# Normalising forgetting-attention heads on the output instead of on the probabilities, for six heads of eight

## The chip, the core and the metric

The kernel runs on one core of a Trainium2 chip. A core has a matrix engine (TensorE, PE in the profile, with its weight loads shown apart as PEld), a vector engine (VectorE, DVE), a scalar engine (ScalarE, ACT), GpSimd (POOL) and SyncE (SP), which here only starts DMAs. The metric is the device time of one execution, in microseconds (us). Lower is better.

## The reference

Two layers, each a feed-forward block, a mixer and a second feed-forward block on 512 tokens of width 1024, in float32. Half of the mixer's heads are forgetting-attention heads (FoX, eight of width 64), the other half differential-attention heads (Diff, four with two score maps each). Only the FoX heads are touched here:

```
s_f = einsum('bhqd,bhkd->bhqk', qf, k_f) * scale_f
s_f = s_f + cf[..., :, None] - cum_f[..., None, :]      # cumulative log forget gates
p_f = softmax(where(causal, s_f, -inf), axis=-1)
o_f = einsum('bhqk,bhkd->bhqd', p_f, v_f)
```

The outputs of all heads are concatenated, multiplied by `w_out` and added to the residual stream. A softmax is an exponential divided by its row sum; since the division is by one number per query, it can be done on the probabilities or on the output of the second product.

## The kernel before, in words

Every large product is made of three matmuls: each factor is split into a rounded high half and a remainder, and high x high, high x low and low x high are added in PSUM (`mm3`, L401 to L403 in the feed-forward and output products, L679 to L681 for the values). The halves come from one copy on ACT (L83) and one subtraction on DVE (L84). Weights stream from DRAM through a ring of tiles, loaded by SP and split as they come.

The mixer (called once per layer) puts its attention work in steps, one head after another: `units` is four Diff heads and then eight FoX heads, and each has four steps, one per block of 128 queries (`qb`) or keys (`kb`). The loop over `s` at the end of `mixer` does in step `s`:

- `trans_step`, for the head that is one unit and a step behind: PE transposes the probabilities of key block `kb` (L888) into a PSUM tile of tag "b", of which there are five; ACT copies the rounded half (L897) and DVE subtracts it (L898).
- `softmax_step`: two matmuls per score tile and one that adds the mask (L838, L839, L841), again into a "b" tile; DVE adds the cumulative gates and finds the row extreme (L874); ACT takes the exponential and, with `accum_out`, its row sum (L876); DVE takes the reciprocal of the sum (L877); ACT multiplies the block by it in place (L878).
- `pv_step`, one step behind `trans_step`: two matmuls against the value halves (L927, L928). After `kb` = 3 the two halves of a head's output sit on different partitions: ACT copies one (L957), DVE adds the other (L958) into `fo["u"]`, a [128, 512] tile that holds two heads, the even one on partitions 0 to 63. After the odd head `split_o` makes the two halves for the output product (L909 on ACT, L910 on DVE).

Between these, `fill_to` lets a generator of other PE work advance to a count written out by hand in `TARGET`: the remaining projections, the values, the gates, and at last the output product of finished heads (`out_early`). The probabilities of two units lie in two tiles `pg` of 2048 columns: columns 0 to 1279 for the four blocks of a unit, 1280 to 1791 for a second map or `fo["u"]`, and 1792 to 2047 unused. Small working tiles come from `t_tile`, a rotation of six.

The order in which an engine runs its instructions is not the order of the program text: the framework builds it ahead of time from the dependencies. On each engine it is then fixed, and an instruction that waits holds up what stands behind it.

The Diff heads already use a way by DRAM for their own norm (`diff_norm`): SP writes a row of numbers to DRAM (L976) and reads it back onto all partitions (L980), and DVE multiplies by it (L982). POOL's DMA queue (L134) carries loads that add onto a tile, for the feed-forward blocks only.

Of the kernel before, what the change touches and what calls it, by code (L numbers as in the profile page):

```python
# [8 lines left out]
F32 = mybir.dt.float32  # L9
F32R = mybir.dt.float32r  # L10
BF16 = mybir.dt.bfloat16
AF = mybir.ActivationFunctionType
ALU = mybir.AluOpType
AX = mybir.AxisListType

P = 128
S = 512
# [5 lines left out]
FOX_H = 8  # L23
DIFF_H = 4
NB = S // P
# [22 lines left out]
def rf(t):  # L48
    return t.bitcast(F32)
# [3 lines left out]
def trunk(ctx, tc, xT, x, gains, gain_row, w_gu, w_dn, w_in, w_ff, w_out, fbias, lams, subln, consts, rope, out):  # L53
    nc = tc.nc
    act, dve, pool, pe, sp = nc.scalar, nc.vector, nc.gpsimd, nc.tensor, nc.sync
# [3 lines left out]
    sm = ctx.enter_context(tc.tile_pool(name="sm", bufs=4))  # L59
    ps = ctx.enter_context(tc.tile_pool(name="ps", bufs=1, space=bass.MemoryType.PSUM))  # L60
    dram = ctx.enter_context(tc.tile_pool(name="dram", bufs=2, space=bass.MemoryType.DRAM))
    turn = {}

    def nxt(key, n):
        i = turn.get(key, 0)
        turn[key] = i + 1
        return i % n
# [4 lines left out]
    def home(tag, shape, dt, name):  # L72
        return sb.tile(shape, dt, tag=tag, name=name, bufs=1)

    def t_tile(shape, dt, name, i=None):
        return home(f"t{nxt('t', 6) if i is None else i}", shape, dt, name)
# [139 lines left out]
    for n in range(2 * DEPTH):  # L216
        l = n // 2
        if n % 2 == 1:
            for i in range(24 + len(OUT_K)):
                k = OUT_K[i - 24] if i >= 24 else None  # L220
                tag = MIX[i % 3] if i < 24 else None if k >= 4 else MIX[(i - 28) % 3]
# [44 lines left out]
    ident = const.tile([P, P], F32, name="ident")  # L266
# [328 lines left out]
    def mixer(l, n_next, mid):  # L595
# [11 lines left out]
        pg = [home(f"G{3 + i}", [P, 2048], F32, f"pg{i}") for i in range(2)]  # L607
        PR = {3: 0, 2: 512, 1: 896, 0: 1152}

        def pr_tile(u, qb):  # L610
            w = (qb + 1) * P
            return pg[u % 2][:, PR[qb]:PR[qb] + w]

        def pm_tile():
            return pg[nxt("pm", 2)][:, 1280:1792]
# [214 lines left out]
        units = [("d", h) for h in range(DIFF_H)] + [("f", h) for h in range(FOX_H)]  # L830
        probs = [[] for _ in units]

        def scores(q1, kk, m, qb, masked):
            n = (qb + 1) * P
            w = max(n, 256)
            p = psum("b")
            lq = q1[m][:, qb * P:n]
            pe.matmul(p[:, 0:w], lq, kk[m][:, 0, 0:w], start=True, stop=False)  # L838
            pe.matmul(p[:, 0:w], lq, kk[m][:, 1, 0:w], start=False, stop=not masked)  # L839
            if masked:  # L840
                pe.matmul(p[:, qb * P:n], identb, maskb, start=False, stop=True)  # L841
            return p

        cbs = {}

        def softmax_step(u, qb):
            kind, h = units[u]
            n = (qb + 1) * P
            st = sm.tile([P, 6], F32, tag="st", name="st", bufs=6)
            if kind == "d":  # L850
                q1, kk = qk[("d", h)]
                pm = []
                for m in range(2):
                    p = scores(q1, kk, m, qb, False)
                    e = pr_tile(u, qb) if m == 0 else pm_tile()
                    dve.tensor_tensor_reduce(out=e[:, 0:n], in0=p[:, 0:n], in1=maskw[:, S - n:S], op0=ALU.add,
                                             op1=ALU.min, scale=1.0, scalar=3.0e38, accum_out=st[:, m:m + 1])
                    act.activation(out=e[:, 0:n], in_=e[:, 0:n], func=AF.Exp, scale=-1.0, bias=st[:, m:m + 1],
                                   accum_out=st[:, 2 + m:3 + m])
                    pm.append(e)  # L860
                dve.reciprocal(out=st[:, 4:6], in_=st[:, 2:4])
                dve.tensor_tensor(out=st[:, 5:6], in0=st[:, 5:6], in1=nlam, op=ALU.mult)
                act.mul(out=pm[1][:, 0:n], in_=pm[1][:, 0:n], mul=st[:, 5:6])
                dve.scalar_tensor_tensor(out=pm[0], in0=pm[0], scalar=st[:, 4:5], in1=pm[1][:, 0:n],
                                         op0=ALU.mult, op1=ALU.add)
                probs[u].append(pm[0])
            else:
                q1, kk = qk[("f", h // 2)]
                if qb == 0:
                    cbs[h] = rope_t[h % 2]  # L870
                    sp.dma_start(out=cbs[h], in_=cum_d[h:h + 1, :].partition_broadcast(P))
                p = scores(q1, kk, h % 2, qb, True)
                e = pr_tile(u, qb)
                dve.tensor_tensor_reduce(out=e, in0=p[:, 0:n], in1=cbs[h][:, 0:n], op0=ALU.add, op1=ALU.min,  # L874
                                         scale=1.0, scalar=3.0e38, accum_out=st[:, 0:1])
                act.activation(out=e, in_=e, func=AF.Exp, scale=-1.0, bias=st[:, 0:1], accum_out=st[:, 2:3])  # L876
                dve.reciprocal(out=st[:, 4:5], in_=st[:, 2:3])  # L877
                act.mul(out=e, in_=e, mul=st[:, 4:5])  # L878
                probs[u].append(e)

        pts = {}
# [1 line left out]
        def trans_step(u, kb):  # L883

            w = S - kb * P
            p = psum("b")
            for qb in range(kb, NB):
                pe.transpose(p[:, (qb - kb) * P:(qb - kb + 1) * P], probs[u][qb][:, kb * P:(kb + 1) * P], ident)  # L888
            if kb == NB - 1:
                th, tl = pt3  # L890
                dst = slice(P, 2 * P)
                full = (th, tl, slice(256, S))
            else:
                th, tl = pair()
                dst = slice(0, w)
                full = (th[:, 0:w], tl[:, 0:w], slice(kb * P, S))
            act.copy(out=th[:, dst], in_=p[:, 0:w])  # L897
            dve.tensor_tensor(out=tl[:, dst], in0=p[:, 0:w], in1=rf(th[:, dst]), op=ALU.subtract)  # L898
            pts[(u, kb)] = full
# [5 lines left out]
        fo = {}  # L905

        def split_o(i, u):
            oh, ol = y_pair(i)
            act.copy(out=oh, in_=u)  # L909
            dve.tensor_tensor(out=ol, in0=u, in1=rf(oh), op=ALU.subtract)  # L910
            ovt[i] = (oh, ol)

        def pv_step(u, kb):
            kind, h = units[u]
            if kb == 0:
                po_[u] = psum("b")
            po = po_[u]
            th, tl, cols = pts.pop((u, kb))
            hs = slice(h * P, (h + 1) * P)
            if kind == "d":  # L920
                vh, vl = vd[kb]
                pe.matmul(po[:, cols], vh[:, hs], th, start=kb == 0, stop=False)
                pe.matmul(po[:, cols], vl[:, hs], th, start=False, stop=False)
                pe.matmul(po[:, cols], vh[:, hs], tl, start=False, stop=kb == NB - 1)
            else:
                v = vf[kb][:, hs]
                pe.matmul(po[:, cols], v, th, start=kb == 0, stop=False)  # L927
                pe.matmul(po[:, cols], v, tl, start=False, stop=kb == NB - 1)  # L928
            if kb < NB - 1:
                return  # L930
            po_.pop(u)
            if kind == "d":
                o = os_[h // 2][:, h % 2]
                act.copy(out=o, in_=po)
                sq = t_tile([P, S], F32, "osq")
                act.activation(out=sq, in_=po, func=AF.Square)
                sh_, sl_ = pair()
                act.copy(out=sh_, in_=sq)
                dve.tensor_tensor(out=sl_, in0=sq, in1=rf(sh_), op=ALU.subtract)
                ov[h] = o  # L940

                def stats():
                    pq = psum("b")
                    pe.matmul(pq[0:32], ones[:, 0:32], sh_, start=True, stop=False)
                    pe.matmul(pq[0:32], ones[:, 0:32], sl_, start=False, stop=True)
                    act.activation(out=vv[32 * h:32 * h + 32], in_=pq[0:32], func=AF.Identity, scale=1.0 / P,
                                   bias=eps_t[0:32])
                    if h == DIFF_H - 1:
                        diff_norm()
                later.append(stats)  # L950
            else:
                if h % 2 == 0:
                    fo["u"] = pm_tile()
                own = slice(64 * (h % 2), 64 * (h % 2) + 64)
                oth = slice(64 - 64 * (h % 2), P - 64 * (h % 2))
                t = t_tile([P, S], F32, "fot")
                act.copy(out=t[own], in_=po[oth])  # L957
                dve.tensor_tensor(out=fo["u"][own], in0=po[own], in1=t[own], op=ALU.add)  # L958
                if h % 2 == 1:
                    split_o(h // 2, fo["u"])  # L960

        later = []
# [135 lines left out]
        for s in range(4 * len(units) + 5 + LAG):  # L1098
            u, i = divmod(s, 4)
# [6 lines left out]
            v, kb = divmod(s - 4 - LAG, 4)  # L1106
# [8 lines left out]
            v, kb = divmod(s - 5 - LAG, 4)  # L1115
# [330 lines left out]
```

## Time and profile before

| | |
|---|---|
| median of three runs | 1860.58 us (1860.45 to 1862.76) |
| profiled execution, device time | 1860.16 us |
| its span, first to last instruction | 1858.2 us |
| granted TensorE clock | 0.998 |
| PE busy | 1829.4 us |
| DVE busy | 1610.3 us |
| ACT busy | 1137.7 us |
| POOL busy | 128.2 us |

The profile describes one execution. Busy times are unions of an engine's instructions. Matmuls are pipelined: they start more often than their durations suggest, so PE can be "busy" and still lose time between two starts. "The chain that ended last" walks back from the last instruction, at each step to what released it or to the instruction before it on its engine. "Windows" give each engine's busy time in stretches of the span, "waits" say who waited for whom, and rows of the timeline give start, duration, engine, line, operation, output and inputs with shapes.

### The profile page before, as it was taken

To read this page: it belongs to the slowest core of one execution; us is meant where nothing else is said; L and a number is where in the kernel's file an instruction comes from. 1 tells how busy PE (TensorE), PEld (TensorE's weight loads), DVE (VectorE), ACT (ScalarE), POOL (GpSimd) and SP (SyncE) were. 2 spreads that over 40 slices of the span, in tenths; PEclk is the share of its full clock that TensorE was granted. 3 is DMA by queue.
4 is the path that set the end of the run, shared out by engine and by line. 5 is a ranking of instruction groups with operands and counts; after the bars stand their busy time and mean duration, and the time that the engine had idled before them with its cause. 6 is when DMAs were issued, how large, how long until landed. Compare 5 with 4: busy or idle time off the path is not lost.

```text
span 1858.2 us, 24541 instructions
## 1 busy us (share of the span) xinstructions
PE 1829.4 (98%) x8702; PEld 1492.4 (80%) x8702; DVE 1610.3 (87%) x2531; ACT 1137.7 (61%) x1819; POOL 128.2 (7%) x154
## 2 busy tenths in 40 slices
PE   9999999999999999999999999999999999999997
PEld 5888888777878889888878988887777788888885
DVE  7898899888686999898998989997787869898998
ACT  7555555557795755565575556545677957455564
POOL 2010000000000100100000000000000000000101
PEclk9999999999999999999999999999999999999999
DMA  9786655243336775777557667543333467756742
GB/s 313 206 229 185 188 141 153 91 125 112 105 115 170 204 204 149 197 204 201 139 167 211 171 160 212 157 128 108 110 112 109 134 167 193 224 132 192 216 116 88
DMA packets 95531, 303.81 MB, mean 164 GB/s; under 512 B 12568, under 2 KB 15128, under 8 KB 95408
## 3 DMA queue, kind: packets, MB, share of 16 engines
q1 hardware_dynamic: 74816, 232.15, 36.9%
q0 software_dynamic: 19296, 68.17, 20.7%
q10 hardware_dynamic: 1296, 1.93, 0.3%
q8 instruction: 68, 1.11, 0.2%
q14 instruction: 55, 0.45, 0.1%
HBM read 287.45 MB, written 2.16 MB: 156 GB/s over the span
## 4 chain that ended last, share of the span: by engine, by line
PE 85%; DVE 8%; ACT 3%; DMA 2%; issue 1%; SPq 0%; DVEq 0%; ACTq 0%
PE ps_c L401 12%; PE ps_c L403 12%; PE ps_c L402 12%; PE ps L403 9%; PE ps L402 9%; PE ps L401 9%; PE ps_a L402 4%; PE ps_a L401 4%; PE ps_a L403 3%; DVE wg L84 2%; PE ps_t L497 2%; DVE x L526 1%; PE ps_g L1265 1%; PE ps_b L888 1%; PE ps_b L838 1%; PE ps_b L839 1%
## 5 line engine op out<-in xcount | busy, mean ns | idle before, releaser
L83 ACT CAST wg<-raw 128x1024 fp32r<-128x1024 f32 (+1 forms) x525 | 537.9, 1032 | 480.8 <-PE ps_c L403 173.0
L84 DVE TENSOR_TENSOR wg<-raw,wg 128x1024 fp32r<-128x1024 f32 (+1 forms) x525 | 621.2, 1194 | 101.1 <-ACT wg L83 96.5
L401 PE MATMUL ps_c<-wg,xf 128*128 128x512 f32 (+1 forms) x736 | 277.7, 378 | 1.7 <-ACT wg L83 1.6
L402 PE MATMUL ps_c<-wg,xf 128*128 128x512 f32 (+1 forms) x736 | 276.5, 376 | 1.4 <-DVE wg L84 1.4
L403 PE MATMUL ps_c<-wg,xf 128*128 128x512 f32 (+1 forms) x736 | 275.7, 375 | 0.0
L401 PE MATMUL ps<-wg,xf 128*128 128x512 f32 (+1 forms) x552 | 210.1, 381 | 0.0
L402 PE MATMUL ps<-wg,xf 128*128 128x512 f32 (+1 forms) x552 | 207.3, 376 | 0.9 <-DVE wg L84 0.9
L403 PE MATMUL ps<-wg,xf 128*128 128x512 f32 (+1 forms) x552 | 206.7, 376 | 0.0
L401 PEld LDWEIGHTS ps_c<-wg,xf 128*128 128x128 f32 x736 | 138.3, 188 | 28.6 <-ACT wg L83 2.5
L402 PEld LDWEIGHTS ps_c<-wg,xf 128*128 128x128 f32 x736 | 138.5, 188 | 27.2 <-DVE wg L84 2.2
L403 PEld LDWEIGHTS ps_c<-wg,xf 128*128 128x128 f32 x736 | 138.5, 188 | 25.0
L134 POOL DMA_DIRECT2D raw<-w_gu x86 | 74.6, 867 | 1129.7 <-DMA raw<-w_gu 628.0
L401 PE MATMUL ps_c<-wg,hf 128*128 128x512 f32 x352 | 138.5, 393 | 4.2 <-DVE x L526 4.0
L402 PE MATMUL ps_c<-wg,hf 128*128 128x512 f32 x352 | 137.4, 390 | 0.0
L403 PE MATMUL ps_c<-wg,hf 128*128 128x512 f32 x352 | 137.1, 390 | 0.0
L526 DVE SCALAR_TENSOR_TENSOR x<-ps_c,x 128x512 f32<-128x512 f32 x192 | 124.8, 687 | 1.3 <-PE ps_c L403 1.2
L402 PEld LDWEIGHTS ps<-wg,xf 128*128 128x128 f32 x552 | 104.0, 188 | 18.9 <-DVE wg L84 1.3
L403 PEld LDWEIGHTS ps<-wg,xf 128*128 128x128 f32 x552 | 103.8, 188 | 18.9
L401 PEld LDWEIGHTS ps<-wg,xf 128*128 128x128 f32 x552 | 104.0, 188 | 17.9 <-ACT xf L83 0.4
L401 PE MATMUL ps_a<-XA,wg 128*128 128x512 f32 x256 | 105.8, 414 | 2.2 <-ACT XA L355 1.8
L402 PE MATMUL ps<-wg,hf 128*128 128x512 f32 x264 | 103.1, 391 | 0.0
L401 PE MATMUL ps<-wg,hf 128*128 128x512 f32 x264 | 103.1, 390 | 0.0
(290 smaller groups left out, 3550.9 us busy)
## 6 DMA issues: line engine op xcount, KB each, us to landing
raw<-w_gu SPq DMA_DIRECT2D x218, 512.0 KB, 4.7
raw<-w_dn SPq DMA_DIRECT2D x100, 512.0 KB, 4.4
raw<-w_gu POOLq DMA_DIRECT2D x86, 512.0 KB, 6.8
raw<-w_in SPq DMA_DIRECT2D x48, 512.0 KB, 3.3
raw<-w_dn POOLq DMA_DIRECT2D x40, 512.0 KB, 5.9
kdup<-qk_t SPq DMA_DIRECT2D x64, 128.0 KB, 2.3
raw<-w_out SPq DMA_DIRECT2D x16, 512.0 KB, 3.2
raw<-w_dn SPq DMA_DIRECT2D x20, 256.0 KB, 3.8
```

The lines of the kernel that those rows point to most:

```text
L83: act.copy(out=hi, in_=src)
L84: dve.tensor_tensor(out=lo, in0=src, in1=rf(hi), op=ALU.subtract)
L134: pool.dma_start(out=t, in_=where(two, h)[1], accum_op=ALU.add)
L401: pe.matmul(p, lh, rh, start=start, stop=False, skip_group_check=again)
L402: pe.matmul(p, lh, rl, start=False, stop=False, skip_group_check=again)
L403: pe.matmul(p, ll, rh, start=False, stop=stop, skip_group_check=again)
L497: pe.transpose(pj[j][:, e * 256 + p * P:e * 256 + (p + 1) * P], hs[j][p][:, o:o + P], ident)
L526: dve.scalar_tensor_tensor(out=xc, in0=src, scalar=scale, in1=xc, op0=ALU.mult, op1=ALU.add)
L838: pe.matmul(p[:, 0:w], lq, kk[m][:, 0, 0:w], start=True, stop=False)
L839: pe.matmul(p[:, 0:w], lq, kk[m][:, 1, 0:w], start=False, stop=not masked)
L888: pe.transpose(p[:, (qb - kb) * P:(qb - kb + 1) * P], probs[u][qb][:, kb * P:(kb + 1) * P], ident)
L1265: pe.matmul(pg[2 * half + j], gained(kp, e, half)[:, j * P:(j + 1) * P], w0[kp][:, e * S:(e + 1) * S], start=kp + e == 0, stop=kp == KP - ...
```

## The change

For FoX heads 0 to 5 (named `LATE`, for the late division) the probabilities stay undivided. The four row sums of a head are collected in one [128, 4] tile. In the head's `trans_step` for `kb` = 1, whose PSUM tile has 128 columns free, PE transposes the sums into those columns, DVE takes the reciprocals there ([4, 128]) into a `t_tile`, and POOL's DMA queue writes them to a DRAM row and reads it back twice, 256 columns each, onto the 64 partitions on which the head's output lies, in the unused columns of `pg`. After the odd head's addition DVE multiplies the pair's [128, 512] output by them in two products of 256 columns, ahead of `split_o`. Heads 6 and 7 are as before.

```
+        LATE = range(FOX_H - 2)
+        sums_ = {}
+        rs_d = dram.tile([FOX_H, S], F32, name="rs_d")
+        rb_h = [t[:, 1792:2048] for t in pg]
+
+        def row_sums(h, p):
+
+            pe.transpose(p, sums_.pop(h), ident)
+            rr = t_tile([P, S], F32, "rr")
+            dve.reciprocal(out=rr[0:NB, 0:P], in_=p)
+            pool.dma_start(out=rs_d[h].rearrange("(q p) -> q p", p=P), in_=rr[0:NB, 0:P])
+            own = slice(64 * (h % 2), 64 * (h % 2) + 64)
+            for c in range(2):
+                pool.dma_start(out=rb_h[c][own], in_=rs_d[h:h + 1, c * 256:c * 256 + 256].partition_broadcast(64))
...
-                act.activation(out=e, in_=e, func=AF.Exp, scale=-1.0, bias=st[:, 0:1], accum_out=st[:, 2:3])
-                dve.reciprocal(out=st[:, 4:5], in_=st[:, 2:3])
-                act.mul(out=e, in_=e, mul=st[:, 4:5])
+                if h in LATE:
+                    if qb == 0:
+                        sums_[h] = sm.tile([P, NB], F32, tag="fsum", name="fsum", bufs=2)
+                    acc = sums_[h][:, qb:qb + 1]
+                else:
+                    acc = st[:, 2:3]
+                act.activation(out=e, in_=e, func=AF.Exp, scale=-1.0, bias=st[:, 0:1], accum_out=acc)
+                if h not in LATE:
+                    dve.reciprocal(out=st[:, 4:5], in_=acc)
+                    act.mul(out=e, in_=e, mul=st[:, 4:5])
...
+            if kb == 1 and units[u][0] == "f" and units[u][1] in LATE:
+                row_sums(units[u][1], p[0:NB, S - P:S])
...
                 if h % 2 == 1:
+                    for c in range(2 if h in LATE else 0):
+                        uc = fo["u"][:, c * 256:c * 256 + 256]
+                        dve.tensor_tensor(out=uc, in0=uc, in1=rb_h[c], op=ALU.mult)
                     split_o(h // 2, fo["u"])
```

## The prediction, made before the change was run

> **What bounds the kernel now.** I read the page first, its busy shares and the chain that ended last, and then the attention stage of one layer by windows.
>
> ```profile
> PE 1829.4 (98%) x8702; PEld 1492.4 (80%) x8702; DVE 1610.3 (87%) x2531; ACT 1137.7 (61%) x1819; POOL 128.2 (7%) x154
> ```
>
> ```profile
> PE 85%; DVE 8%; ACT 3%; DMA 2%; issue 1%; SPq 0%; DVEq 0%; ACTq 0%
> ```
>
> PE holds 85% of the chain, so nothing taken off ACT counts unless PE was waiting for it. The windows (busy us of PE, weight load, DVE, ACT, POOL) cover the FoX heads of the first layer in three parts, and the middle part of the second layer.
>
> ```profile
> 460.00:510.00 50.00, 50.00 (x259) 40.34 (x258) 31.76 (x85) 37.03 (x78) 0.00 (x0) 1.00 0.32 103
> 510.00:560.00 50.00, 48.35 (x256) 36.99 (x256) 45.12 (x116) 45.83 (x109) 0.00 (x0) 1.00 0.35 110
> 560.00:590.00 30.00, 30.00 (x144) 24.28 (x143) 13.44 (x22) 13.49 (x26) 3.45 (x4) 1.00 0.89 245
> ...
> 1430.00:1480.00 50.00, 48.55 (x258) 37.53 (x258) 45.01 (x115) 45.80 (x108) 0.00 (x0) 1.00 0.37 111
> ```
>
> Only the middle part can give anything back. Before it, and after it, PE is busy throughout; in it ACT (45.83 of 50) and DVE (45.12 of 50) are both near full and PE pauses. The second layer repeats the first to 0.2 us. What the weight loads wait for in 510 to 560 (total, times, longest):
>
> ```profile
> PEld ps_b L888 <- ACT pg L878: 1.6, 3, 0.7
> PEld ps_b L928 <- DVE pair L898: 0.8, 1, 0.8
> PEld ps_a L402 <- DVE XA L84: 0.7, 1, 0.7
> PEld ps_a L401 <- DVE qk_t L804: 0.6, 1, 0.6
> PEld ps_b L927 <- ACT pair L897: 0.6, 3, 0.3
> PEld ps_b L888 <- DVE pg L958: 0.5, 1, 0.5
> PEld ps_b L838 <- ACT qk L787: 0.2, 1, 0.2
> PEld ps_a L401 <- ACT XA L83: 0.2, 1, 0.2
> ```
>
> L878 is the multiplication that the change removes for six heads. A load's idle time is not yet lost PE time:
>
> ```profile
> 516.44 0.39 PE L403 MATMUL ps_a<-XA,wg 128*128 128x512 f32 x1
> ...
> 516.66 0.39 PE L401 MATMUL ps_a<-XA,wg 128*128 128x512 f32 x1
> ...
> 517.17 0.14 PEld L888 LDWEIGHTS ps_b<-ident,pg 128*128 128x128 f32 x1 [0.54 <-ACT pg L878]
> 517.17 0.33 PE L888 MATMUL ps_b<-ident,pg 128*128 128x128 f32 x1
> ```
>
> Matmuls follow one another at 0.22 to 0.23 us although each lasts 0.39. Here the next one came 0.51 us later, so 0.28 us were lost beside a load idle of 0.54: about half. I take half of each such row.
>
> **The change, part by part.** The sum is made against the profiled execution, 1860.16 us (a span of 1858.2 and 2.0 around it); the median of the three runs shown, 1860.58, is 0.42 higher.
>
> *Removed.* Six heads of eight, four blocks each, two layers: 48 multiplications on ACT and 48 reciprocals on DVE.
>
> ```profile
> L878 ACT ACTIVATE pg<-pg,st 128x128 f32<-128x128 f32 (+1 forms) x64 | 34.7, 561 | 5.6 <-DVE st L877 5.2
> ```
>
> ```profile
> L877 DVE RECIPROCAL st<-st 128x1 f32<-128x1 f32 x64 | 9.8, 158 | 7.3 <-ACT pg L876 7.1
> L328 DVE RECIPROCAL nst<-nst 128x4 f32<-128x4 f32 x6 | 1.1, 176 | 2.3 <-ACT nst L327 2.3
> L742 DVE RECIPROCAL zt<-zt 128x32 f32<-128x32 f32 x2 | 0.7, 342 | 0.0
> L1275 DVE TENSOR_TENSOR acc<-acc,sq 128x256 f32<-128x256 f32 x14 | 5.9, 422 | 3.1 <-ACT sq L1273 3.1
> ```
>
> ACT loses 48 x 0.561 = 26.9 us of work. That is a large number worth little: half of L878's 1.6 us, and half of L897's 0.6 (ACT casts that now queue behind less), is 1.1 us of PE per layer, **-2.2 us** in all. The bounds are 0, if DVE is late in ACT's place, and -5.2, half of all eight rows (5.2) in both layers.
>
> *PE adds* a transpose of the four sums per head, 12 in all.
>
> ```profile
> 451.03 0.44 PE ps_b L888 x4
> ```
>
> On the chain four transposes take 0.44 us, so 0.11 each and 12 x 0.11 = **+1.3 us**, whole, since PE is the bound; they run beside three other transposes of the same step. The upper bound is a full unpipelined duration, about 0.33 as in the row at 517.17, or 4 us. A gain is excluded: the instruction is new on the busiest engine.
>
> *DVE adds* per head a reciprocal over 128 elements of four partitions. The rows at 1, 4 and 32 elements rise by (342 - 176) / 28 = 5.9 ns per element, so 342 + 96 x 5.9 = 0.91 us by extension, against 0.42 if it cost only what an ordinary operation of 256 columns does. Per pair it adds two products of 128x256, 0.42 each by L1275. Over the kernel that is 12 x 0.91 + 12 x 0.42 - 48 x 0.158 = +8.4 us of DVE. In 510 to 560 fall the reciprocals of heads 2 to 5 (3.6), three pairs' products (2.5), and 14 removed reciprocals (2.2): net +3.9, on a DVE with 4.9 idle. Of that idle, these two rows are not ACT's and stay:
>
> ```profile
> DVE pg L874 <- PE ps_b L841: 1.1, 4, 0.6
> DVE ou L982 <- DMA rbd<-ms_d: 0.6, 1, 0.6
> ```
>
> 45.1 + 3.9 + 1.7 = 50.7 us for a stretch of 50: 0.7 per layer, **+1.4 us**. The bounds are 0 (the last pair's product slips behind 560, where DVE is busy 13.4 of 30) and +7.8 (nothing absorbed). The reciprocal also reads the PSUM bank of the step for 0.91 us longer, one of five; I cost that at nothing while four others turn over.
>
> *DMA adds* per head one write of 2 KB and two broadcasts of 64 KB, all on POOL's queue: 18 issues per layer. POOL is idle until 569 (0.00 in the first two windows), so nothing of its own is delayed; SP's queue is untouched. The `rr` tile moves the rotation of the six t tiles on by one per head, at no cost as long as its write is read before six more allocations. The products on DVE wait for the landings, and behind them on DVE stand the evictions (L804), the transposed halves (L898), and the weight halves (L84), for all of which the rows above show PE waiting. The nearest chain in the trace is the Diff heads' norm, issued from SP:
>
> ```profile
> 503.18 2.48 DMA ms_d<-nd
> 505.67 3.24 DMA rbd<-ms_d
> ...
> 512.12 3.64 DMA rbd<-ms_d
> ```
>
> ```profile
> raw<-w_gu SPq DMA_DIRECT2D x218, 512.0 KB, 4.7
> ...
> raw<-w_gu POOLq DMA_DIRECT2D x86, 512.0 KB, 6.8
> ```
>
> Reciprocal, write and broadcast give 0.91 + 2.48 + 3.24 = 6.6 us at the least, and 2.1 more for each of two DMAs from POOL (6.8 against 4.7; that difference also holds an accumulation) 10.8 at the most. What is available runs from the step's first cast to the end of the odd head's output addition:
>
> ```profile
> 506.22 0.46 ACT L897 CAST pair<-ps_b 128x384 fp32r<-128x384 f32 x1
> ...
> 530.96 0.48 ACT L897 CAST pair<-ps_b 128x384 fp32r<-128x384 f32 x1
> ...
> 548.01 0.48 ACT L897 CAST pair<-ps_b 128x384 fp32r<-128x384 f32 x1
> ```
>
> ```profile
> 522.65 0.69 DVE L958 TENSOR_TENSOR pg<-ps_b,fot 64x512 f32<-64x512 f32 x1
> ...
> 529.53 0.15 DVE L634 TENSOR_SCALAR sub_s<-subln_sb 128x1 f32<-128x1 f32 x1
> ...
> 537.06 0.69 DVE L958 TENSOR_TENSOR pg<-ps_b,fot 64x512 f32<-64x512 f32 x1
> ...
> 556.71 0.69 DVE L958 TENSOR_TENSOR pg<-ps_b,fot 64x512 f32<-64x512 f32 x1
> ```
>
> For heads 2 and 3: 537.75 - 530.96 = 6.8 us; for heads 4 and 5: 557.40 - 548.01 = 9.4; for heads 0 and 1, 523.34 - 506.22 = 17.1. The broadcasts of head 4 overwrite what the product of heads 2 and 3 reads, and so wait for it on POOL; head 5's three issues stand behind them, but come 8 us later. So the wait lies between 0 and 4.0 + 1.4 per layer. I take 0.6 for heads 2 and 3 alone, **+1.2 us**, by the row of L982: DVE's order is not the program's order (L634 is written at the head of the mixer and runs at 529.53), and where a DVE operation consumes a small broadcast now, it was placed late enough to wait 0.6.
>
> A rule of the Trainium skill bears on this chain. The page "DMA: Bandwidth & Descriptors", section "Anatomy of one DMA", puts a DMA from GpSimd at about 2.0 us plus bytes over 436 GB/s. By it the chain would be an estimated 0.91 + 2.0 + 2.15 = 5.1 us, plus a second issue, under the 6.8, and this term 0. For 512 KB it would give 3.2 us, where the row has 6.8, so I don't lean on it; no row here shows so small a DMA from POOL.
>
> **The sum.** -2.2 + 1.3 + 1.4 + 1.2 = +1.7 us: 1861.9 on the profiled execution's scale, **1862.3 us** beside the median. 0.2% of the time, about what a measurement of this kernel can tell from no change, is 3.7 us. So: no change.
>
> **Rivals.** *A, DVE stands waiting for a broadcast: slower.* The product sits at the head of DVE's queue and PE follows. It decides once the chain is longer than 8.4 us: -2.2 + 1.3 + 1.4 + 2 x (8.4 - 6.8) = 3.7. At 9.7 the wait is 2.9 + 0.3 = 3.2 per layer, 6.4 in place of 1.2: +6.9, 1867.5; at the upper end +11.3, 1871.9. For it: only 6.8 us are available. Against it: the small waits on DMAs so far.
>
> POOL's issue row bears on this as well:
>
> ```profile
> L134 POOL DMA_DIRECT2D raw<-w_gu x86 | 74.6, 867 | 1129.7 <-DMA raw<-w_gu 628.0 <-DVE wg L84 154.5 <-DVE x L526 105.5
> ```
>
> Three issues are 2.6 us inside the chain, and none of them looks stretched by a busy DVE (mean 867 ns). The Trainium skill's page "SBUF — State Buffer", section "Who interferes with whom", warns that a DMA from GpSimd starves while DVE runs a two-port operation, but says that `tensor_tensor` is inferred not to cause this; the issue row agrees with that. Were the inference wrong here, each issue could be held by one L84, which would be this rival.
>
> *B, ACT was all that held PE: faster.* DVE fits into the idle time that ACT leaves, and all eight PE waits go: -5.2 + 1.3 = -3.9, 1856.7. For it: ACT's 45.8 of 50 falls by 14 x 0.56 = 7.9. Against it: four of the eight rows name DVE, with 2.6 of the 5.2 us, which gets fuller.
>
> *C, DVE becomes the bound without any wait: slower.* Its extra 3.9 us per layer come whole: -2.2 + 1.3 + 7.8 + 1.2 = +8.1, 1868.7. For it: 49.0 of 50. Against it: 16.6 us of DVE idle time right after 560.
>
> **How the numbers follow.** Forecast 0.56, A 0.20, B 0.12, C 0.12. The forecast's own range is 1858 to 1864. Ends of 1857 and 1869 leave out most of B and the upper part of A, about 2 in 10. Faster by over 0.2% is B: 0.12; within it, the forecast: 0.56; slower, A and C: 0.32.
>
> **What would show it.** In the profile after, ACT in 510 to 560 should fall to about 38; L878 should count 16, and no weight load should wait for it with heads 2 to 5. The new reciprocal should read about 0.9 us. DVE should stand at 48 to 49 of 50 in that stretch, with a wait for the broadcast of at most 1 us per layer: 2 us or more would be A, and DVE full without it C. I would be wrong if the chain through DRAM took over 8.4 us, if the new reciprocal were far from 0.9, or if ACT's time came back to PE whole.

## The result, and the profile after

The changed kernel takes 1871.43 us (median of four runs, 1869.21 to 1872.68) against 1861.31 (four runs of the kernel before beside them): 10.1 us slower, a ratio of 1.0054 with a 95% interval of 1.0041 to 1.0067. The forecast was 1862.3, the range 1857 to 1869. The profiled execution took 1870.82 us, its span 1868.1.

The lines below follow the prediction's order. In the kernel after, all line numbers behind L851 have moved: the exponential is L897 (was L876), the gate addition L889 (L874), the multiplication L900 (L878), the transposes L910 (L888), ACT's cast L921 (L897), DVE's subtraction L922 (L898), the value matmuls L951 and L952 (L927, L928), the output addition L982 (L958), the two halves of an output L933 and L934 (L909, L910). New are L853 (transpose of the sums), L855 (reciprocal), L856 and L859 (POOL's DMAs) and L986 (products).

The page, busy times and the chain that ended last:

```profile
PE 1835.3 (98%) x8714; PEld 1496.7 (80%) x8714; DVE 1618.3 (87%) x2507; ACT 1117.7 (60%) x1771; POOL 147.3 (8%) x190
```

```profile
PE 83%; DVE 10%; ACT 3%; DMA 2%; issue 1%; SPq 0%; DVEq 0%; ACTq 0%; POOL 0%; POOLq 0%
```

DVE rose by 8.0 us (8.4 was forecast), ACT fell by 20.0 (the 48 multiplications last 27.0 in sum, but in part beside other work of ACT), and on the chain two per cent went from PE to DVE. The groups of the operations that the change touches:

```profile
L900 ACT ACTIVATE pg<-pg,st 128x128 f32<-128x128 f32 (+3 forms) x16 | 8.6, 558 | 0.3 <-DVE st L899 0.2
L855 DVE RECIPROCAL rr<-ps_b 4x128 f32<-4x128 f32 x12 | 11.3, 942 | 0.1
L921 ACT CAST pair<-ps_b 128x256 fp32r<-128x256 f32 (+2 forms) x72 | 33.4, 475 | 22.6 <-PE ps_b L910 15.9 <-DVE rr L855 6.0
L853 PE MATMUL ps_b<-ident,fsum 128*4 128x128 f32 x12 | 3.3, 272 | 0.0
```

The multiplication counts 16, as it should, and the new reciprocal takes 942 ns (0.91 us was extrapolated). The third row is a surprise: ACT's cast stood idle for 6.0 us until that reciprocal was done.

The windows of the FoX heads (busy us of PE, weight load, DVE, ACT, POOL; behind them the granted clock, DMA share, GB/s):

```profile
460.00:510.00 50.00, 50.00 (x259) 40.42 (x258) 31.83 (x77) 32.45 (x69) 1.65 (x3) 1.00 0.31 99
510.00:560.00 50.00, 46.70 (x238) 35.42 (x238) 45.18 (x101) 36.09 (x85) 7.84 (x15) 0.97 0.41 122
560.00:590.00 30.00, 29.93 (x145) 23.90 (x143) 15.54 (x30) 14.49 (x28) 3.55 (x4) 1.00 0.83 244
...
1430.00:1480.00 50.00, 45.57 (x230) 34.15 (x230) 43.51 (x92) 33.44 (x77) 6.27 (x12) 0.97 0.40 120
```

The whole loss lies in the middle part, in both layers: PE ran 238 matmuls there in place of 256. Outside the mixers nothing is lost: the additions of the feed-forward blocks (L526 in both kernels) run 0.2 us earlier than before just ahead of the first mixer, 4.7 later behind it, 4.6 later ahead of the second and 10.1 later behind that. DVE is the instructive column. It was to fill up to 48 or 49 of 50 and stands at 45.18, as before (45.12), although it was given more work: it did less of the stretch's work in the same time, so its busy share in a fixed window did not rise. ACT stands at 36.09 (about 38 was forecast). And the granted clock, 1.00 before, is 0.97.

What the weight loads wait for from 510 to 560 us:

```profile
PEld ps_b L952 <- DVE pair L922: 2.1, 4, 0.9
PEld ps_b L951 <- ACT pair L921: 2.0, 3, 0.9
...
PEld ps_b L838 <- ACT qk L787: 0.7, 1, 0.7
PEld ps_a L402 <- DVE XA L84: 0.7, 2, 0.5
```

No load waits for the multiplication with a late head any more. In its place stand the two halves of the transposed probabilities, 0.8 and 0.6 us before. No row anywhere names a wait of a product for a broadcast. The timeline of the worst place, heads 3 and 4:

```profile
539.96 0.69 DVE L982 TENSOR_TENSOR pg<-ps_b,fot 64x512 f32<-64x512 f32 x1
...
540.69 0.95 DVE L855 RECIPROCAL rr<-ps_b 4x128 f32<-4x128 f32 x1
...
541.66 0.42 DVE L986 TENSOR_TENSOR pg<-pg,pg 128x256 f32<-128x256 f32 x1
541.72 0.48 ACT L921 CAST pair<-ps_b 128x384 fp32r<-128x384 f32 x1 [0.56 <-DVE rr L855]
542.01 0.42 DVE L986 TENSOR_TENSOR pg<-pg 128x256 f32<-128x256 f32 x1
542.25 0.44 PE L951 MATMUL ps_b<-pair,vf 128*128 128x384 f32 x1 [0.74 <-ACT pair L921]
542.34 0.55 DVE L922 TENSOR_TENSOR pair<-ps_b,pair 128x384 fp32r<-128x384 f32 x1
...
542.95 0.44 PE L952 MATMUL ps_b<-pair,vf 128*128 128x384 f32 x1 [0.26 <-DVE pair L922]
...
544.36 0.39 PE L952 MATMUL ps_b<-pair,vf 128*128 128x256 f32 x1 [0.74 <-DVE pair L922]
```

Output addition, reciprocal and both products run one behind the other on DVE; ACT's cast waits for the second, DVE's subtraction for all, and PE for cast and subtraction. Then a second thing happens:

```profile
547.49 0.63 PE L403 MATMUL ps_a<-XA,y 128*128 128x512 f32 x1
...
547.92 0.63 PE L402 MATMUL ps_a<-XA,y 128*128 128x512 f32 x1
548.34 0.44 PE L403 MATMUL ps_a<-XA,y 128*128 128x512 f32 x1
548.62 0.39 PE L402 MATMUL ps_a<-XA,y 128*128 128x512 f32 x1
548.85 0.40 PE L403 MATMUL ps_a<-XA,y 128*128 128x512 f32 x1
```

The matmuls stand 0.43 us apart and last 0.63, then go back to 0.23 and 0.39. The windows say why:

```profile
546.00:548.00 2.00, 2.00 (x7) 1.54 (x6) 0.96 (x2) 0.94 (x3) 0.00 (x0) 0.50 0.83 226
```

Behind the pause the granted clock is 0.50. Summed over windows of 2 us, what the clock lacks of 1.00 comes to 3.42 us, 1.71 in each layer; before, it lacks nothing in either attention stage.

### The profile page after: what moved, and what is told of

It is laid out like the page before. It is cut to its first block, busy times and chain, and to the rows that moved or that the text cites. A ratio compares the mean times of both kernels' runs of the same rounds, so it can differ in the third digit from the quotient of the medians.

```text
span 1868.1 us, 24597 instructions
## 1 busy us (share of the span) xinstructions
PE 1835.3 (98%) x8714; PEld 1496.7 (80%) x8714; DVE 1618.3 (87%) x2507; ACT 1117.7 (60%) x1771; POOL 147.3 (8%) x190
## 4 chain that ended last, share of the span: by engine, by line
PE 83%; DVE 10%; ACT 3%; DMA 2%; issue 1%; SPq 0%; DVEq 0%; ACTq 0%; POOL 0%; POOLq 0%
PE ps_c L401 12%; PE ps_c L403 12%; PE ps_c L402 12%; PE ps L402 9%; PE ps L403 9%; PE ps L401 9%; PE ps_a L401 3%; PE ps_a L402 3%; PE ps_a L403 3%; DVE wg L84 2%; PE ps_t L497 2%; PE ps_g L1292 1%; DVE x L526 1%; PE ps_b L910 1%; ACT wg L83 1%
## 5 line engine op out<-in xcount | busy, mean ns | idle before, releaser
L526 DVE SCALAR_TENSOR_TENSOR x<-ps_c,x 128x512 f32<-128x512 f32 x192 | 124.3, 683 | 1.3 <-PE ps_c L403 1.2
```

What stands on the lines that cost most here:

```text
L526: dve.scalar_tensor_tensor(out=xc, in0=src, scalar=scale, in1=xc, op0=ALU.mult, op1=ALU.add)
```

## The experiments

Three theories stood at the start. **Load**: DVE's new work delays PE wherever it stands. **Bank**: the reciprocal reads the PSUM tile of its step, and cast and PE stand behind it. **DRAM**: the products wait for broadcasts, or the transfers disturb others. All times are medians; the kernel before took 1861.2 to 1861.8 us beside them. One caution holds for all: the framework rebuilds the order of the instructions for each kernel, so a small difference can be order. How much a new order costs by itself no run measures; two runs that only move the same work differ from their base by 2.3 and 2.6 us, and the argument rests on larger differences.

**The removal alone.** No transpose or reciprocal of the sums, no transfers, no products.

```
-                row_sums(units[u][1], p[0:NB, S - P:S])
...
-                        dve.tensor_tensor(out=uc, in0=uc, in1=rb_h[c], op=ALU.mult)
```

> Leaves out the division of heads 0 to 5 altogether: no multiplication on the probabilities, no sums' transpose, reciprocal, DMA or product (the outputs of these heads stay undivided). Before is 1861.3 us, the change 1871.4. All three theories put the loss into what the change adds, so all expect this to fall to or below before: 1856 to 1861, the lower end if ACT's relief comes back to PE (rival B's 5.2 us). A time near 1870 would say that the loss comes from a rearranged order and not from the added work.

Measured 1854.99 us, ratio 0.9964 (0.9952 to 0.9977): the removal gives 6.2 us, so what is added costs 16.4. The window from 535 to 550 us, to which the following runs come back, first with the removal alone and then in the changed kernel:

```profile
535.00:550.00 15.00, 15.00 (x87) 12.10 (x85) 14.40 (x36) 12.55 (x32) 0.00 (x0) 1.00 0.63 193
```

```profile
535.00:550.00 15.00, 12.70 (x55) 8.69 (x54) 13.39 (x29) 9.38 (x24) 2.65 (x6) 0.89 0.33 99
```

87 matmuls and 55, in the same 15 us.

**Reciprocal behind the cast.** The transpose stays; reciprocal and DMAs are emitted after cast and subtraction of the step.

> The sums' transpose stays where it is, but the reciprocal and its DMAs are written behind ACT's cast and DVE's subtraction of key block 1, which read the same PSUM tile. Theory 'bank' (ACT's cast stands behind the 0.94 us reciprocal, and PE behind the cast): half of the 10.1 us or more comes back, 1866 or less. Theory 'load' (the added DVE time costs wherever it stands): 1870 to 1872. Theory 'DRAM' (the products wait for the broadcasts, or the broadcasts slow other copies): 1871 or more, since the chain starts later.

Measured 1869.15 us, ratio 1.0042 (1.0028 to 1.0055). 2.3 us back: "bank" is not the main cause.

**Short reciprocal.** It is taken on the [128, 4] sums before their transpose; ACT copies the transposed row out of PSUM behind the cast.

```
-            dve.reciprocal(out=rr[0:NB, 0:P], in_=p)
+            act.copy(out=rr[0:NB, 0:P], in_=p)
...
+                dve.reciprocal(out=sm_, in_=sm_)
+                pe.transpose(p[0:NB, S - P:S], sm_, ident)
```

> The reciprocal is taken of the [128, 4] sums before their transpose (0.18 us by the row of L328, in place of 0.94) and ACT copies the transposed row to SBUF behind the cast. 'Bank': 1862 to 1866, as with the reciprocal behind the cast or a little better. 'Load': DVE gets back 12 x 0.76 = 9.1 us, eight of the twelve in the full stretches, about 6 us, so 1864 to 1867. 'DRAM': 1869 to 1871, the chain is only 0.5 us shorter.

Measured 1861.52 us, ratio 0.9999 (0.9991 to 1.0008). With all transfers and products in place, 9.9 us come back: the 0.94 us reciprocals make most of the loss, and no theory had expected so much. (The short ones stand behind the cast besides; that alone gave 2.3.) The short one (minimum, median, maximum in ns, then the first and last start):

```profile
L921 DVE RECIPROCAL fsum<-fsum x12: 160/170/178, 478.3 to 1466.4; 128x4 f32<-128x4 f32 x12
```

**No transfers.** The products multiply by a constant tile.

> As the change, but without its three DMAs per head: the products multiply by a tile that POOL sets to 1 once per layer (the outputs of heads 0 to 5 stay undivided, the reciprocals go nowhere). 'DRAM': most of the 10.1 us comes back, 1864 or less. 'Bank' and 'load': 1869 to 1872, since the reciprocal and the products stand where they stood.

Measured 1868.3 us, ratio 1.0036 (1.0024 to 1.0049): 3.1 us back, nearer to "load" than to "DRAM".

**Each addition alone**, on top of the removal: first the twelve reciprocals, reading SBUF and used by nothing; then the twelve products by a constant.

```
+                rr = t_tile([P, S], F32, "rr")
+                dve.reciprocal(out=rr[0:NB, 0:P], in_=probs[u][NB - 1][0:NB, P:2 * P])
```

> Leaves out the division of heads 0 to 5: like the kernel with the removal alone (1855.0 us), but with the twelve reciprocals of [4, 128], now read from SBUF (from the head's own probabilities) and used by nothing; no transposes of sums, no transfers, no products. By the load theory their 11.3 us of DVE stand ahead of subtractions for which PE waits, wherever they read from: 1863 to 1865. By the bank theory a reciprocal that reads no PSUM holds up neither the cast nor the bank: 1855 to 1857. By the DRAM theory also 1855 to 1857, since nothing goes by DRAM.

> Leaves out the division of heads 0 to 5: like the kernel with the removal alone (1855.0 us), but with the twelve products of 128x256, by a constant tile that is there from the start; no sums, reciprocals or transfers. By the load theory their 5.0 us of DVE come to 3 to 5 us: 1858 to 1860. If the products cost only when they wait for a broadcast (DRAM theory): 1855 to 1856. If only the reciprocals stand in a bad place: 1855 to 1856 as well.

Measured 1861.45 us (0.9999, 0.999 to 1.0008) and 1856.04 (0.9969, 0.9958 to 0.9981): 6.5 and 1.1 us over the removal. Reciprocals that read no PSUM still cost 6.5; neither outcome is quite what "load" gave.

**Both together, and the reciprocal in PSUM without products.**

> Leaves out the division of heads 0 to 5: the twelve reciprocals reading SBUF and the twelve products by a constant together, with neither transposes nor transfers. Alone they cost 6.5 us and 1.1 us over the removal alone (1855.0). If DVE time simply adds up: 1862 to 1863. If the two together make a longer stretch of DVE work ahead of the subtraction that PE waits for (burst theory): 1865 or more. By the bank theory, which needs the reciprocal to read PSUM, not over 1863.

> Leaves out the division of heads 0 to 5: the transposes of the sums and the reciprocals reading the PSUM tile as in the change, with neither transfers nor products. With transfers away and products there it was 1868.3 us. If the place of the operand counts (the cast of the step stands behind the reciprocal): 1866 to 1868. If it does not, and the products made the difference: 1862 to 1863.5, the SBUF reciprocals (1861.5) and 1.3 for the transposes.

Measured 1867.3 us (1.0029, 1.0018 to 1.0039) and 1865.7 (1.0022, 1.0014 to 1.0031). Together the two cost 12.3 us, not 7.6: they do not add up, which spoke for a fourth theory, **burst**: a long row of DVE work ahead of a subtraction that PE waits for. The second run lies 4.2 above the SBUF reciprocals, of which I put 1.3 down to the transposes: some 2.9 us for reading the step's PSUM tile, just under what was expected for it. With the products there, the same two things together add only 1.0 (1868.3 against 1867.3), so the share of "bank" is not settled. The clock in the first (535 to 550 us):

```profile
535.00:550.00 15.00, 12.13 (x47) 8.49 (x46) 12.70 (x27) 7.95 (x22) 0.00 (x0) 0.77 0.44 130
```

and with the reciprocals alone:

```profile
535.00:550.00 15.00, 12.56 (x67) 9.27 (x66) 14.64 (x28) 9.96 (x23) 0.00 (x0) 1.00 0.48 142
```

20 matmuls fewer in 15 us, at a granted clock of 0.77: in both layers together the clock lacks 5.1 us there and nothing with the reciprocals alone, about as much as the 4.7 us by which the sum fails. No run holds the clock up to test this.

**The reciprocal a step later**, without transfers: the same work, with the reciprocal of head 4 out of the row at 540 us.

```
-            if kb == 1 and units[u][0] == "f" and units[u][1] in LATE:
+            if kb == 2 and units[u][0] == "f" and units[u][1] in LATE:
```

> Leaves out the division of heads 0 to 5: the kernel without transfers (1868.3 us), with the transpose of the sums and the reciprocal in the step of key block 2 in place of 1. The work is the same, but the reciprocal of head 4 no longer stands between the output addition and the products of heads 2 and 3, with the subtraction for which PE waits behind all four. By the burst theory the pause at 540 us and the halved clock after it go (3.4 us), and some of the waiting: 1862 to 1865. By the load theory, to which the order is nothing: 1867 to 1869.

Measured 1865.68 us, ratio 1.0019 (1.001 to 1.0028): 2.6 us back, between the two. The clock still falls, in one layer of two (1.70 us). Inconclusive.

**Fewer heads**, with the long reciprocal: two, four, and four others.

```
-        LATE = range(FOX_H - 2)
+        LATE = range(2)
```

> Computes the whole reference. The change as it was, with its long reciprocal, but for heads 0 and 1 alone; heads 2 to 7 keep the division on the probabilities. If what counts is the place (DVE has 18 of 50 us idle up to 510 us, and the reciprocals of heads 0 and 1 stand at 505 to 520): within 1 us of the kernel before, 1860.5 to 1862.5. If every long reciprocal and product costs the same wherever it stands: a third of 10.1, so 1864.5 to 1865.

> Computes the whole reference. The change as it was, for heads 0 to 3 alone. The products of heads 2 and 3 stay, with their transfers, but head 4 has no reciprocal that would stand beside them. By the burst theory the clock is not halved and PE pauses less: 1861 to 1864. If every pair of heads past the first costs the same: 1861.0 + half of 10.4 = 1866.

> Computes the whole reference. The change for heads 0, 1, 4 and 5; heads 2, 3, 6 and 7 keep the division on the probabilities. Two pairs as in the run with heads 0 to 3 (1870.7 us), the same work added. If what decides is the stretch from 535 to 550 us, in which the products of heads 2 and 3 stand beside the last projections (place): 1861 to 1864. If each pair past the first costs its DVE time (load): 1866 to 1871.

Measured: heads 0 and 1, 1861.02 us (0.9996, 0.9988 to 1.0005); heads 0 to 3, 1870.73 (1.0049, 1.0037 to 1.0062); heads 0, 1, 4 and 5, 1861.58 (1.0005, 0.9996 to 1.0014). The second lies above both expectations and contradicts "burst" as I had put it: no reciprocal stands between the addition and the products of heads 2 and 3 there, and the loss is whole. The third settles it against "load": the same number of heads, the same operations, 9.1 us apart. It is the pair of heads 2 and 3, whose reciprocals and products fall into the stretch up to 550 us. The two runs also relieve ACT of other heads' multiplications; that this does not make the difference is shown by the next run, which has the relief of heads 0 to 3 and no loss. That stretch with heads 0 to 3:

```profile
535.00:550.00 15.00, 13.13 (x62) 9.34 (x60) 12.76 (x37) 13.98 (x36) 1.57 (x3) 0.89 0.39 113
```

and with heads 0, 1, 4 and 5:

```profile
535.00:550.00 15.00, 13.83 (x76) 9.56 (x76) 13.51 (x28) 12.33 (x30) 1.56 (x3) 1.00 0.41 117
```

62 matmuls against 76, with the clock at 0.89 and at 1.00, though the second has a long reciprocal in this stretch as well:

```profile
538.97 0.94 DVE L855 RECIPROCAL rr<-ps_b 4x128 f32<-4x128 f32 x1
```

With heads 0 to 3, PE waits for DVE's subtractions, which stand behind the products, and for the keys of the next heads (L787), which come late:

```profile
544.72 0.39 PE L952 MATMUL ps_b<-pair,vf 128*128 128x256 f32 x1 [0.40 <-DVE pair L922]
...
545.52 0.38 PE L952 MATMUL ps_b<-pt,vf 128*128 128x256 f32 x1 [0.31 <-DVE pt L922]
546.58 0.58 PE L838 MATMUL ps_b<-qk 128*128 128x256 f32 x1 [0.67 <-ACT qk L787]
```

**Heads 0 to 3 with the short reciprocal.** Products and transfers stay.

> Computes the whole reference. Heads 0 to 3 divided late, with the short reciprocal of [128, 4]: the products and the transfers stay as in the run with the long one (1870.7 us), only the reciprocal's 0.94 us goes. If the long reciprocals of heads 2 and 3 made the loss: 1859 to 1863. If the products or the transfers of that pair did: 1867 or more.

Measured 1858.67 us, ratio 0.9985 (0.9976 to 0.9994): 12.1 us below the same heads with the long one.

```profile
535.00:550.00 15.00, 14.48 (x80) 11.13 (x79) 14.55 (x41) 14.90 (x37) 0.00 (x0) 1.00 0.61 168
```

80 matmuls, and DVE busier (14.55) than with the long one (12.76). Eight reciprocals of 0.94 us, 7.5 us in all, make 12.1 in this place, less what standing behind the cast is worth (not measured for four heads); up to 3.4 of them are the halved clock.

**Which part of the removal gave 6.2 us?** The multiplications go, the short reciprocals stay on DVE, unused.

```
-                act.mul(out=e, in_=e, mul=st[:, 4:5])
+                if h >= FOX_H - 2:
+                    act.mul(out=e, in_=e, mul=st[:, 4:5])
```

> Leaves out the division of heads 0 to 5, as the removal alone does (1855.0 us), but keeps their 48 short reciprocals on DVE; only the 48 multiplications on ACT are gone. If what the removal gave, 6.2 us, was ACT standing in PE's way: 1855 to 1856. If it was the 7.6 us of DVE: 1860 to 1861.5. A sum of both shares lies between.

Measured 1855.23 us, ratio 0.9964 (0.995 to 0.9977). All of the gain is ACT's; taking the 48 short reciprocals off DVE gave nothing that can be measured.

**Other ways to divide late.** First the short reciprocal with the products on POOL; then no DRAM at all: one reciprocal of [128, 8] per pair, an ACT copy that repeats each sum 64 times, four transposes into a PSUM tile, one product by it; then that for all eight heads, and with reciprocal and copy two steps earlier.

```
+                        dve.reciprocal(out=rs, in_=rs)
+                        rt = t_tile([P, S], F32, "rt")
+                        act.copy(out=rt.rearrange("p (x d) -> p x d", d=64),
+                                 in_=rs.rearrange("p (x o) -> p x o", o=1).broadcast_to([P, 2 * NB, 64]))
+                        pb = psum("b")
+                        for qb in range(NB):
+                            pe.transpose(pb[:, qb * P:qb * P + P], rt[:, qb * P:qb * P + P], ident)
+                        dve.tensor_tensor(out=fo["u"], in0=fo["u"], in1=pb, op=ALU.mult)
```

> Computes the whole reference. The kernel with the short reciprocal (1861.5 us), with the twelve products on POOL in place of DVE. By the load theory DVE is freed of 5.0 us: 1857 to 1859. Rivals: the product is slower on POOL and what follows it (the split, the output product) comes late, or POOL slows DVE down while both run: 1861.5 or more.

> Computes the whole reference, without DRAM: per pair one short reciprocal of [128, 8], one ACT copy that repeats each sum 64 times along a row, four transposes into a PSUM tile and one product of 512 columns by it. From the removal alone, 1855.0, plus 24 transposes of 0.11 (2.6) and 1.1 for the products: 1858 to 1860. Rival: addition, product and split of the odd head stand in one row on DVE, with a PSUM tile of five held meanwhile, and PE waits behind them as in the change: 1862 or more.

> Computes the whole reference: the same for all eight heads, so that no division is left on the probabilities. By the load theory heads 6 and 7 free ACT further and add 0.9 us of transposes: 1858 to 1860. Rival: the last pair's output is needed at once by the output product, and the longer way to it delays PE: 1 to 2 us more than with six heads.

> Computes the whole reference: the kernel with the broadcast on PE (1857.3 us), with its reciprocal and its repeating ACT copy two steps earlier, in the odd head's step of key block 2. There a load waits 0.7 us for that copy and another 0.4 behind it. If these waits are real loss: 1855.5 to 1856.8. If not, 1857 to 1858.

Measured 1863.29 us with the products on POOL (1.0011, 1.0002 to 1.002), 1857.31 with the broadcast on PE (0.998, 0.997 to 0.9989), 1858.58 for all heads (0.9985, 0.9977 to 0.9994) and 1857.74 with the earlier copy (0.998, 0.9971 to 0.9989). POOL is no relief. The broadcast on PE beats both kernels, the one before by 4.2 us. It adds matmuls to the engine that bounds the kernel, and PE hardly loses by it:

```profile
535.00:550.00 15.00, 14.76 (x87) 11.65 (x85) 14.08 (x36) 13.91 (x31) 0.00 (x0) 1.00 0.54 162
```

87 matmuls, as with the removal alone. An earlier copy gains nothing, so the loads' waits for it were not lost time.

## Why the prediction was wrong

The medians give a ladder from the kernel before to the changed one: -6.2 (removal), +12.3 (reciprocals and products on DVE), +1.0 (transposes, and PSUM in place of SBUF), +3.1 (transfers), in sum +10.2 where 10.1 was measured. Against it, the steps of the prediction:

- **ACT relief, "-2.2", bounds 0 to -5.2.** Right in kind, mis-sized: -6.4 with the multiplications alone gone. I had taken half of the waits that name ACT. But those that name DVE became fewer too (2.6 us before, 0.6 with the removal alone), probably because the subtraction stands behind ACT's cast. With the removal alone PE is busy 15.00 of 15 from 535 to 550 us, 14.04 before. So rival B's ceiling was too low as well.

```profile
535.00:550.00 15.00, 14.04 (x72) 9.97 (x71) 13.25 (x34) 14.81 (x38) 0.00 (x0) 1.00 0.49 151
```

- **Transposes, "+1.3".** Not measured by themselves. The kernel with 24 transposes on PE lies 2.3 us over the removal, products included; that is 0.10 for each, so 0.11 was not too little.
- **DVE's addition, "+1.4", bounds 0 to +7.8: the step that failed.** Its parts were right (0.94 us for 0.91, DVE +8.0 for +8.4); its place on the path was not. I set net 3.9 us against 4.9 idle in a window of 50 and charged the excess. The runs show 12.3 for the reciprocals and products together, on top of the removal; the 48 short reciprocals that the sum credited to DVE were worth nothing (1855.23 us with them, 1854.99 without). DVE's idle time in that stretch was no room: the rows at 541 us show PE, ACT and DVE waiting for one another in a circle (transpose, cast, subtraction, product), and a reciprocal of 0.95 us ahead of a cast holds up the round. Heads 2 and 3 and the length of the reciprocals make the loss: heads 0 to 3 take 1870.73 us with long ones and 1858.67 with short ones. With heads 0, 1, 4 and 5 the kernel takes as long as before; what their reciprocals cost may be covered by ACT's relief there, since no run has these heads without them. The upper bound assumed that at the worst the added time comes whole; the clock's loss, up to 5.1 us in the run with 12.3, can come on top.
- **The PSUM bank, "I cost that at nothing while four others turn over".** Wrong in kind: not the turning over of banks but ACT's cast of the same tile waited, 6.0 us in all. What it costs PE is not settled: some 2.9 us without the products, nothing beyond the transposes with them, 2.3 by moving the reciprocal behind the cast.
- **Transfers, "+1.2" for one wait per layer of the products.** That wait is in no row, so rival A did not happen. The transfers cost 3.1 us all the same, by the run without them; where is not settled. The copies of the keys on SP's queue land late at times (up to 4.9 us, before 2.4), but do so without the transfers too (4.4).
- **The halved clock** was in no step: up to 3.4 of the 10.1 us. The runs of the changed kernel fit this: 1869.21 us at a mean granted clock of 0.997, 1872.05 and 1872.68 at 0.995.

Rival C, "DVE becomes the bound without any wait", came near with 1868.7, but its sign of recognition, a full DVE, is not there (45.18 of 50), and its price took every window of DVE alike, where one stretch of 15 us per layer decides. Rival A's upper end, 1871.9, hits the number by luck: its wait did not happen. What stays open is why the pair of heads 2 and 3 costs its whole loss with and without head 4's reciprocal beside its products. That pair and the length of its reciprocals are shown as the cause; which wait comes first, and how much of it is the new order that the framework builds around a long reciprocal, is not.

## What to carry to other kernels

An engine's idle time in a wide window need not be room for new work: here the window held a loop in which the bound engine waits for it. Take the stretch in which PE pauses already, and ask there what stands behind the new instruction. A [4, 128] operation is not a small one: put the statistics across partitions (four elements each) before the reciprocal, and the same reciprocals take 0.17 us in place of 0.94. And where short pauses of PE come close together, price a halved clock behind them too: here it lacked 1.71 us each time.

## What the runs showed of the hardware

- **The clock falls without a long idle time.** In the changed kernel no single pause of PE at 540 us exceeds 1.0 us. Counting each matmul at its distance from the next at full clock, those between 541.35 and 544.76 us fill 0.21 of 3.41 us. The Trainium skill, page "TensorE: Matmul & The Clock Gate", section "Part 1: The HAM clock gate (the "warmup" mystery)", has a gate of two states, half and full, that goes by free-running windows of about 3.4 us, and puts the fall after an idle one. The trace agrees with the half (0.50) and the length (halved from 545.01 to 548.42 us, 3.41 us); it differs in that the window was not idle. In the attention stages of all kernels together the clock fell eleven times. How full such a window must be to keep the clock is not shown: counted in the same way, it fell behind one filled to about 0.35 (reciprocals in SBUF with products, at 542.26 us) and stayed behind one filled to 0.25 to 0.30, by where the window is laid (the changed kernel, at 347 us).
- **Small DMAs from POOL** were issued in 0.52 and 0.53 us:

```profile
L856 POOL DMA_DIRECT2D rs_d<-rr x12 | 6.2, 519 | 458.1 <-DVE rr L855 439.6 <-DVE st L899 18.5
L859 POOL DMA_DIRECT2D pg<-rs_d x24 | 12.7, 534 | 20.7 <-DMA rs_d<-rr 10.4 <-DVE y L934 5.4 <-PE ps_b L968 3.3
```

where the loads that add onto a tile take 0.87; from issue to landing the write of 2 KB took 1.6 us and the broadcasts of 64 KB 2.8 (medians), shorter than the bounds I had taken.
